# Second mixer: the products between token halves as whole matmuls, those of the two coarsest levels as 64 by 64 tiles

## The chip, the cores and the metric

The kernel runs on one core of one Trainium2 chip. The metric is the device time of one execution in microseconds; the time of the kernel before is 2440.34 us, the median of three runs (2439.63 to 2445.22).

A core has engines that run their own streams of instructions side by side: TensorE (matmuls, PE in the profile; its weight loads stand apart as PEld), VectorE (DVE), ScalarE (ACT), GpSimd (POOL) and SyncE (SP, which here issues most transfers). They meet through semaphores. Matmul results go to PSUM, everything else lies in SBUF, and the weights come from device memory by DMA.

## The reference

The reference is a trunk of two layers over 256 tokens of width 2048, in float32. Each layer adds a token mixer and then a gated MLP with a convolution of width 3; RMS norms stand before each, and one closes the trunk. The first layer's mixer is an mLSTM, the second layer's an HGRN2 recurrence, run forward and backward over the tokens with 16 heads of width 128. The change concerns the second alone:

```python
def _hgrn_chunk(s_st, xs):
    q, k, lf, v = xs
    b = jnp.cumsum(lf, axis=2)
    rel = jnp.where(lower[:, :, None], b[:, :, :, None, :] - b[:, :, None, :, :], -jnp.inf)
    attn = jnp.einsum('bhtsk,bhsk->bhts', jnp.exp(rel) * q[:, :, :, None, :], k)
    o = jnp.einsum('bhts,bhsv->bhtv', attn, v) + jnp.einsum('bhtk,bhkv->bhtv', q * jnp.exp(b), s_st)
    ...
y = hgrn_direction(q, k_f, lf_f, v) + fl(hgrn_direction(fl(q), fl(k_b), fl(lf_b), fl(v)))
```

Every pair of tokens t and s has a weight: the sum over 128 channels of q at t times k at s times the decays of all tokens between them, forward for s before t and backward for s after t. The output of a head is that 256 by 256 matrix times V.

## The kernel before

All large products are streamed. `stream` walks a list of chunks, 1 MB pieces of weights come in through SyncE's queue, ScalarE and VectorE split each piece into a rounded part and a rest (`wh` in L147, `wl` in L148), and TensorE multiplies both with the activations. In chunks of kind "tm" three matmuls of 512 columns follow each other (L192, L193, L194); in chunks of kind "fm" one of 512 and one of 256 (L202, L209). These are the regular matmuls.

Work of the mixer itself is put between them. `side.tick` counts a planned time with every regular matmul and steps generators that have become due (`Side`, L85 to L113). What a generator issues between two regular matmuls is a visit of TensorE here. A scheduler with a simulated clock then makes the final order of each engine's stream: it goes by the program's order, but lets a ready instruction pass one that isn't ready in its simulation. So a transpose of an earlier head (L767) can stand inside a visit.

The second mixer does a head in `head(hd)` (L666 to L751). The decay between two tokens is built by levels of 1, 2, 4, 8, 16, 32 and 64 tokens: at each level VectorE multiplies blocks of the tiles QZ and KZ by a factor from G (L706, L707), GpSimd halves G (L712), and `gather` copies the blocks of a level into a pair of tiles, keys and queries, called kq (L686). After the last level comes the visit. It forms the matrix of weights, keys on partitions and queries on columns:

- between the two halves of 128 tokens, straight from QZ and KZ: four matmuls for each direction, each with 32 keys as the weights and 128 queries as columns, written to 32 partitions of the PSUM tile `pa` (L718 to L723);
- for the two coarsest levels (ms[6] and ms[5]): `product` with 8 matmuls each, 32 keys against 64 queries, to `pa` (L724, L725);
- for the five finer levels and the diagonal (ks and q): `product` with 8 matmuls each, 32 keys against 32 queries, to `pd` (L726 to L728).

Then ScalarE copies `pd` to AD (L729), VectorE puts the levels together under masks (L731), ScalarE copies `pa` to AT (L732) and the diagonal blocks from AD into it (L735). About ten microseconds later four matmuls multiply AT with V (L746), the result is scaled, and `finish` transposes it (L767). The data are float32, which TensorE takes in two passes: one such matmul of the source stands in the profile as two weight loads and two matmuls. The 16 heads follow each other; the visit of a head is one of 16.

Of the kernel before, what the change touches and what calls it, by code (L numbers as in the profile page):

```python
# [15 lines left out]
P = 128  # L16
T = 256
# [31 lines left out]
QUAD = 32  # L49
# [6 lines left out]
def trunk_kernel(ctx, tc, xT, x_d, fg_d, pp_d, cst_d, w_first, w_aq, w_ak, w_av, w_ao, w_aout,  # L56
                 w_bq, w_bv, w_bg, w_bout, w_up, w_down, out, mscr):
    nc = tc.nc
    act, dve, pool, pe = nc.scalar, nc.vector, nc.gpsimd, nc.tensor
# [21 lines left out]
    def aux(name):  # L81
        return psa.tile([P, 512], F32, tag="aux", name=name)
# [283 lines left out]
    def head_scale(ss, width):  # L366
        rs = ev.tile([P, 2], F32, tag="rs", bufs=6, name="rs")
        dve.tensor_scalar(rs, ss, 1.0 / width, EPS, ALU.mult, ALU.add)
        pool.tensor_tensor(rs, rs, hmx, ALU.pow)
        return rs  # L370
# [235 lines left out]
    def hgrn(norm, nxt):  # L606
# [25 lines left out]
        def blocks(z, h, a, b):  # L632
            v = z[:, 0:2 * (T + h)].rearrange("k (p x) -> k p x", p=2)[:, :, a:b]
            return v.rearrange("k p (m j) -> k m p j", j=2 * h)[:, :, :, 0:h]

        def gview(g, n, start, h):
            v = g[:, start:start + 2 * (n - 1)].rearrange("k (p x) -> k p x", p=2)[:, :, 0::2]
            return v.rearrange("k p m -> k m p").unsqueeze(3).broadcast_to([P, n // 2, 2, h])

        def take(hd, what, ps):  # L640
            mp = box["mp"]
            st = heads[hd]
            if what == 0:
                st["q"] = mp.tile([P, T], F32, tag="q", bufs=2, name="q")
                fm_scaled(ps, norm.R, st["q"], box["oml"][:, hd:hd + 1])
                st["QK"] = mp.tile([P, 1152], F32, tag="QK", bufs=2, name="QK")
                st["G"] = mp.tile([P, 768], F32, tag="G0", bufs=2, name="G")
                return
            dr = what - 1
            lb, oml = box["lb"], box["oml"]  # L650
            QZ, KZ, G = st["QK"][:, 0:512], st["QK"][:, 512:1024], st["G"]
            z = mp.tile([P, T], F32, tag="z", bufs=2, name="z")
            fm_scaled(ps, norm.R, z)
            g = G[:, dr * T:(dr + 1) * T]
            kz = KZ[:, dr * T:(dr + 1) * T]
            act.activation(g, z, AF.Sigmoid)
            act.activation(kz, z, AF.Sigmoid, scale=-1.0)
            dve.tensor_scalar(g, g, oml[:, hd:hd + 1], lb[:, hd:hd + 1], ALU.mult, ALU.add)
            pool.tensor_tensor(QZ[:, (1 - dr) * T:(2 - dr) * T], st["q"], g, ALU.mult)
            if dr == 0:  # L660
                pool.tensor_copy(G[:, 512:768], g)
            else:
                st["ks"] = mp.tile([P, T], F32, tag="ks", bufs=2, name="ks")
                pool.tensor_tensor(st["ks"], KZ[:, 0:T], KZ[:, T:2 * T], ALU.add)
                side.push(head(hd))

        def head(hd):
            mp = box["mp"]
            st = heads[hd]
            while hd and "done" not in heads[hd - 1]:  # L670
                yield 0.3
            QZ, KZ = st["QK"][:, 0:640], st["QK"][:, 512:1152]
            q, ks, G = st["q"], st["ks"], st["G"]
            AT = mp.tile([P, 4, P], F32, tag="AT", bufs=2, name="AT")
            AD = mp.tile([P, 2, QUAD], F32, tag="AD", bufs=2, name="AD")

            def gather(h):

                i = box["turn"] % (4 + MIX)
                box["turn"] += 1  # L680
                if i < 4:
                    m = keep.tile([P, 2, T], F32, tag=f"yt{KT - 4 + i}", name=f"kq{i}")
                else:
                    m = mp.tile([P, 2, T], F32, tag="kq", bufs=MIX, name="kq")
                for j, z in enumerate((KZ, QZ)):
                    dve.tensor_copy(m[:, j].rearrange("k (m p j) -> k m p j", p=2, j=h), blocks(z, h, 0, T))  # L686
                return m[:, 0], m[:, 1]

            def product(pd, k, q, n, at):

                for b in range(8):
                    o, c, t = b % 4 * QUAD, b // 4 * pd.shape[1] // 2, at(b)
                    c += t % P if pd.shape[1] == T else 0
                    pe.matmul(pd[o:o + QUAD, c:c + n], k[:, b * QUAD:(b + 1) * QUAD], q[:, t:t + n], start=True, stop=True)  # L694

            def both(ps):
                return ps.rearrange("p (a b) -> p a b", a=2)

            step = SPREAD if hd < BH - 2 else STEP
            mask = [cst[:, C_LV + i * QUAD:C_LV + (i + 1) * QUAD].bitcast(I32).unsqueeze(1).broadcast_to([P, 2, QUAD])  # L700
                    for i in range(FINE)]
            ms, n = [gather(1)], T
            yield step
            for li, h in enumerate(LEVELS):
                qa, ka = blocks(QZ, h, 0, T), blocks(KZ, h, 0, T)
                dve.tensor_tensor(ka, ka, gview(G, n, 1, h), ALU.mult)  # L706
                dve.tensor_tensor(qa, qa, gview(G, n, n + 1, h), ALU.mult)  # L707
                if h < 64:
                    ms.append(gather(2 * h))
                    n //= 2  # L710
                    G2 = mp.tile([P, 3 * n], F32, tag=f"G{h}", bufs=2, name="G2")
                    pool.tensor_tensor(G2, G[:, 0:6 * n:2], G[:, 1:6 * n:2], ALU.mult)  # L712
                    G = G2
                else:
                    st["done"] = True
                yield step
            pa, pd = aux("pa"), aux("pd")
            for b in range(4):  # L718
                o = slice(b * QUAD, (b + 1) * QUAD)
                pe.matmul(pa[o, 2 * P:3 * P], KZ[:, b * QUAD:(b + 1) * QUAD], QZ[:, T + P:2 * T], start=True, stop=True)  # L720
            for b in range(4):
                o, k = slice(b * QUAD, (b + 1) * QUAD), T + P + b * QUAD
                pe.matmul(pa[o, 3 * P:4 * P], KZ[:, k:k + QUAD], QZ[:, 0:P], start=True, stop=True)  # L723
            product(pa[:, 0:T], *ms[6], 64, lambda b: (b // 2 ^ 1) * 64)  # L724
            product(pa[:, 0:T], *ms[5], 64, lambda b: b // 2 * 64)  # L725
            for i in reversed(range(FINE)):  # L726
                product(pd[:, (i + 1) * 64:(i + 2) * 64], *ms[i], QUAD, lambda b: b * QUAD)
            product(pd[:, 0:64], ks, q, QUAD, lambda b: b * QUAD)  # L728
            act.copy(AD, both(pd[:, 0:64]))  # L729
            for i in range(FINE):  # L730
                dve.copy_predicated(AD, mask[i], both(pd[:, (i + 1) * 64:(i + 2) * 64]))  # L731
            act.copy(AT, pa.rearrange("p (a b) -> p a b", a=4))  # L732
            for j in range(4):
                o = slice(j * QUAD, (j + 1) * QUAD)
                act.copy(AT[o, 0:2, o], AD[o])  # L735
            yield
            while "V" not in st["qd"]:
                yield
            V, j = st["qd"]["V"], hd % 4
            py = aux("py")  # L740
            y = mp.tile([P, T], F32, tag="y", bufs=4, name="y")
            ss = mp.tile([P, 2], F32, tag="ss", bufs=2, name="ss")
            for t in range(2):
                c = slice(t * P, (t + 1) * P)
                for s in range(2):
                    pe.matmul(py[:, c], AT[:, s if s == t else 2 + s], V[:, s, j * P:(j + 1) * P], start=(s == 0), stop=(s == 1))  # L746
            act.copy(y, py[:, 0:T])
            for t in range(2):
                jk = ev.tile([P, 512], F32, tag="jk", bufs=1, name="jk")
                act.activation(jk[:, 0:P], y[:, t * P:(t + 1) * P], AF.Square, accum_out=ss[:, t:t + 1])  # L750
            st["y"] = (y, head_scale(ss, 128))  # L751
# [113 lines left out]
    c, close0 = ffn(0, n1, n2)  # L865
    chunks += c
    c = hgrn(n2, n3)
    b = c[0].before
# [6 lines left out]
    c, close1 = ffn(1, n3, nf)  # L875
# [85 lines left out]
```

## Time and profile before

| what | value |
|---|---|
| median of three runs | 2440.34 us (2439.63 to 2445.22) |
| the profiled execution's own time | 2440.68 us |
| its span | 2438.6 us |
| mean granted TensorE clock | 0.998 |
| TensorE busy in the second mixer, 1099 to 1640 us | 537.7 of 541 us |
| VectorE busy there | 456.3 us |
| ScalarE busy there | 283.4 us |
| instruction packets of queue q8 there | 39 of 115 |

The span is the time from the first to the last recorded instruction; the profiled execution's time has 2.1 us around it. The profile names a group of instructions by its line in the kernel, its engine, the tiles it writes and reads, and its shape: `128*32 128x64` is a matmul of 128 rows by 32 columns of weights with 64 columns of data. In a timeline, records of the same kind that follow each other are merged: the row has the first start, the time from it to the last end, and their count. Ends of matmuls are modelled and overlap the next start; starts are measured.

### The profile page before, as it was taken

How to read it: one execution, taken by the hardware profiler on the slowest of the kernel's cores; microseconds unless marked ns; L12 is line 12 of the kernel's file. 1: busy time of each engine (PE TensorE's matmuls, PEld its weight loads, DVE VectorE, ACT ScalarE, POOL GpSimd, SP SyncE). 2: the span in 40 equal slices, each digit the busy share in tenths (PEclk: the TensorE clock that was granted, in tenths of full speed). 3: DMA queues.
4: the chain of work that ended last, by engine and by line, in shares of the span. 5: the costliest groups of instructions: out<-in, count | busy, mean ns of one | idle time of the engine just before them, and what ended most of it. 6: DMA issues, size and time to landing. Idle time of an engine off the chain costs nothing.

```text
span 2438.6 us, 37099 instructions
## 1 busy us (share of the span) xinstructions
PE 2422.2 (99%) x14767; PEld 2068.0 (85%) x14767; DVE 1692.7 (69%) x2768; ACT 1208.0 (50%) x1831; POOL 160.9 (7%) x219
## 2 busy tenths in 40 slices
PE   9999999999999999999999999999999999999998
PEld 7888888888888888888888888888888888888887
DVE  7766556777645777657887988885677754677754
ACT  6655455444434444445554555545544443444443
POOL 0100000000000000001222222220000000000000
PEclk9999999999999999999999999999999999999999
DMA  7654555555555555555544554455555555555554
GB/s 288 199 180 160 186 177 186 190 190 190 191 197 184 188 190 186 183 192 184 173 163 167 173 172 159 172 178 194 183 190 190 190 193 197 185 185 188 190 185 143
DMA packets 66205, 451.90 MB, mean 185 GB/s; under 512 B 7648, under 2 KB 8160, under 8 KB 13424
## 3 DMA queue, kind: packets, MB, share of 16 engines
q1 hardware_dynamic: 63792, 442.91, 53.4%
q0 software_dynamic: 1232, 5.31, 0.9%
q8 instruction: 115, 1.88, 0.3%
q10 hardware_dynamic: 1008, 1.32, 0.2%
q14 instruction: 58, 0.48, 0.1%
HBM read 447.35 MB, written 2.16 MB: 184 GB/s over the span
## 4 chain that ended last, share of the span: by engine, by line
PE 97%; DVE 1%; issue 1%; ACT 0%; DMA 0%; SPq 0%; POOLq 0%; POOL 0%; ACTq 0%
PE mm L202 36%; PE mm L209 18%; PE mm L192 13%; PE mm L194 13%; PE mm L193 13%; PE pn L508 1%; PE pd L694 1%; PE py L746 1%; PE pz L276 0%; DVE wl L148 0%; PE S L494 0%; PE pa L694 0%; DMA raw<-in_w_first 0%; PE pa L720 0%; DVE QK L706 0%
## 5 line engine op out<-in xcount | busy, mean ns | idle before, releaser
L148 DVE TENSOR_TENSOR wl<-raw,wh 128x1024 fp32r<-128x1024 f32 (+1 forms) x848 | 1032.2, 1219 | 594.3 <-ACT wh L147 584.1
L202 PE MATMUL mm<-xt,wh 128*128 128x512 f32 x3776 | 1326.6, 396 | 0.0
L147 ACT CAST wh<-raw 128x1024 fp32r<-128x1024 f32 (+1 forms) x848 | 881.2, 1041 | 879.0 <-PE mm L194 401.6
L209 PE MATMUL mm<-xt,wl 128*128 128x256 f32 x3776 | 1058.1, 280 | 1.8 <-issue 1.8
L202 PEld LDWEIGHTS mm<-xt,wh 128*128 128x128 f32 x3776 | 709.1, 188 | 167.9 <-issue 2.0
L209 PEld LDWEIGHTS mm<-xt,wl 128*128 128x128 f32 x3776 | 712.5, 189 | 2.1
L194 PE MATMUL mm<-wh,g 128*128 128x512 f32 x674 | 262.8, 390 | 0.0
L192 PE MATMUL mm<-wh,g 128*128 128x512 f32 x674 | 262.6, 390 | 0.0
L193 PE MATMUL mm<-wl,g 128*128 128x512 f32 x674 | 262.3, 389 | 0.0
L192 PE MATMUL mm<-wh,xt 128*128 128x512 f32 x512 | 201.2, 396 | 2.7 <-ACT xt L214 2.2
L193 PE MATMUL mm<-wl,xt 128*128 128x512 f32 x512 | 200.9, 392 | 0.4 <-DVE wl L148 0.4
L194 PE MATMUL mm<-wh,xt 128*128 128x512 f32 x512 | 199.9, 392 | 0.0
L219 ACT COPY b<-mm 128x256 f32<-128x256 f32 x237 | 87.8, 370 | 175.4 <-PE mm L209 175.4
L194 PEld LDWEIGHTS mm<-wh,g 128*128 128x128 f32 x674 | 126.5, 188 | 26.6
L193 PEld LDWEIGHTS mm<-wl,g 128*128 128x128 f32 x674 | 126.5, 188 | 26.2
L192 PEld LDWEIGHTS mm<-wh,g 128*128 128x128 f32 x674 | 126.5, 188 | 26.1
L192 PEld LDWEIGHTS mm<-wh,xt 128*128 128x128 f32 x512 | 95.6, 188 | 23.1 <-ACT xt L214 2.9
L193 PEld LDWEIGHTS mm<-wl,xt 128*128 128x128 f32 x512 | 96.5, 188 | 20.0 <-DVE wl L148 0.8
L194 PEld LDWEIGHTS mm<-wh,xt 128*128 128x128 f32 x512 | 96.4, 188 | 19.8
L220 DVE TENSOR_TENSOR a<-mm,b 128x256 f32<-128x256 f32 x86 | 36.5, 425 | 54.3 <-ACT b L219 54.3
L686 DVE COPY kq<-QK 128x256 f32<-128x256 f32 x224 | 70.9, 337 | 0.0
L712 POOL TENSOR_TENSOR G<-G 128x384 f32<-128x384 f32 (+2 forms) x96 | 67.8, 707 | 6.3
(204 smaller groups left out, 1825.4 us busy)
## 6 DMA issues: line engine op xcount, KB each, us to landing
raw<-in_w_up SPq DMA_DIRECT2D x172, 1024.0 KB, 5.0
raw<-in_w_down SPq DMA_DIRECT2D x80, 1024.0 KB, 4.8
raw<-in_w_bq SPq DMA_DIRECT2D x48, 1024.0 KB, 5.0
raw<-in_w_ao SPq DMA_DIRECT2D x16, 1024.0 KB, 4.8
raw<-in_w_aout SPq DMA_DIRECT2D x16, 1024.0 KB, 4.8
raw<-in_w_bv SPq DMA_DIRECT2D x16, 1024.0 KB, 4.8
raw<-in_w_bg SPq DMA_DIRECT2D x16, 1024.0 KB, 4.8
raw<-in_w_bout SPq DMA_DIRECT2D x16, 1024.0 KB, 4.8
```

The lines of the kernel that those rows point to most:

```text
L147: act.copy(wh[:, :m], r)
L148: dve.tensor_tensor(wl[:, :m], r, wh[:, :m].bitcast(F32), ALU.subtract)
L192: pe.matmul(ps[t], xh, wh[:, c], start=st, stop=False)
L193: pe.matmul(ps[t], xh, wl[:, c], start=False, stop=False)
L194: pe.matmul(ps[t], xl, wh[:, c], start=False, stop=sp)
L202: pe.matmul(ps[f], wh[:, c:c + P], x, start=st, stop=False)
L209: pe.matmul(ps[f][:, 0:T], wl[:, c:c + P], x[:, 0:T], start=False, stop=sp)
L219: act.copy(b, ps[:, T:2 * T])
L220: dve.tensor_tensor(dst, ps[:, 0:T], b, ALU.add)
L508: pe.matmul(pn[:, 0:258], w, v, start=(i == 0), stop=(i == len(parts) - 1))
L686: dve.tensor_copy(m[:, j].rearrange("k (m p j) -> k m p j", p=2, j=h), blocks(z, h, 0, T))
L712: pool.tensor_tensor(G2, G[:, 0:6 * n:2], G[:, 1:6 * n:2], ALU.mult)
```

## The change

The four matmuls per direction between token halves become one each, with 128 keys as the weights. `product` gets a width w, 64 for the two coarsest levels and 32 (QUAD) for the others: it walks blocks of w keys, against the w queries of the same block or of its neighbour (`flip`), and writes w partitions. A visit has 2 + 2 x 4 + 6 x 8 = 58 matmuls of the source in place of 4 + 4 + 2 x 8 + 6 x 8 = 72. What is computed for the masked blocks stays the same, and nothing on other engines changes.

```diff
-            def product(pd, k, q, n, at):
-
-                for b in range(8):
-                    o, c, t = b % 4 * QUAD, b // 4 * pd.shape[1] // 2, at(b)
-                    c += t % P if pd.shape[1] == T else 0
-                    pe.matmul(pd[o:o + QUAD, c:c + n], k[:, b * QUAD:(b + 1) * QUAD], q[:, t:t + n], start=True, stop=True)
+            def product(pd, k, q, w, flip=None):
+
+                for b in range(T // w):
+                    o, e = b * w % P, b ^ (flip or 0)
+                    c = b * w // P * pd.shape[1] // 2 + (0 if flip is None else e * w % P)
+                    pe.matmul(pd[o:o + w, c:c + w], k[:, b * w:(b + 1) * w], q[:, e * w:(e + 1) * w], start=True, stop=True)
...
-            for b in range(4):
-                o = slice(b * QUAD, (b + 1) * QUAD)
-                pe.matmul(pa[o, 2 * P:3 * P], KZ[:, b * QUAD:(b + 1) * QUAD], QZ[:, T + P:2 * T], start=True, stop=True)
-            for b in range(4):
-                o, k = slice(b * QUAD, (b + 1) * QUAD), T + P + b * QUAD
-                pe.matmul(pa[o, 3 * P:4 * P], KZ[:, k:k + QUAD], QZ[:, 0:P], start=True, stop=True)
-            product(pa[:, 0:T], *ms[6], 64, lambda b: (b // 2 ^ 1) * 64)
-            product(pa[:, 0:T], *ms[5], 64, lambda b: b // 2 * 64)
+            pe.matmul(pa[:, 2 * P:3 * P], KZ[:, 0:P], QZ[:, T + P:2 * T], start=True, stop=True)
+            pe.matmul(pa[:, 3 * P:4 * P], KZ[:, T + P:2 * T], QZ[:, 0:P], start=True, stop=True)
+            product(pa[:, 0:T], *ms[6], 64, 1)
+            product(pa[:, 0:T], *ms[5], 64, 0)
             for i in reversed(range(FINE)):
-                product(pd[:, (i + 1) * 64:(i + 2) * 64], *ms[i], QUAD, lambda b: b * QUAD)
-            product(pd[:, 0:64], ks, q, QUAD, lambda b: b * QUAD)
+                product(pd[:, (i + 1) * 64:(i + 2) * 64], *ms[i], QUAD)
+            product(pd[:, 0:64], ks, q, QUAD)
```

## The prediction

> **What bounds the kernel now.** I read the page first, then the timeline of one visit on TensorE, then every place where TensorE paused in the second mixer (1099 to 1640 us of the span).
>
> ```profile
> span 2438.6 us, 37099 instructions
> PE 2422.2 (99%) x14767; PEld 2068.0 (85%) x14767; DVE 1692.7 (69%) x2768; ACT 1208.0 (50%) x1831; POOL 160.9 (7%) x219
> ...
> q8 instruction: 115, 1.88, 0.3%
> ...
> PE 97%; DVE 1%; issue 1%; ACT 0%; DMA 0%; SPq 0%; POOLq 0%; POOL 0%; ACTq 0%
> ```
>
> TensorE is the bound: 99% busy, 97% of the chain that ended last. So a nanosecond taken from or added to its stream is a nanosecond of the end, as long as nothing makes it wait. The q8 line comes back below: 115 packets brought instructions. 14767 matmul records and as many weight loads, 29534 together, make 257 to a packet. "Issue", 1% of the chain, is waiting that no operand explains.
>
> A regular visit, from the timeline of TensorE (start us, duration us, line, how many merged):
>
> ```profile
> 1171.03 0.39 PE L193 MATMUL mm<-wl,xt 128*128 128x512 f32 x1
> 1171.26 0.39 PE L194 MATMUL mm<-wh,xt 128*128 128x512 f32 x1
> 1171.58 0.43 PE L720 MATMUL pa<-QK 128*32 128x128 f32 x8
> 1171.82 0.40 PE L723 MATMUL pa<-QK 128*32 128x128 f32 x8
> 1172.04 0.63 PE L694 MATMUL pa<-kq 128*32 128x64 f32 x32
> 1172.48 0.87 PE L694 MATMUL pd<-kq 128*32 128x32 f32 x78
> ...
> 1173.20 0.32 PE L694 MATMUL pd<-q,ks 128*32 128x32 f32 x14
> 1173.45 0.50 PE L192 MATMUL mm<-wh,xt 128*128 128x512 f32 x1
> 1173.79 0.40 PE L193 MATMUL mm<-wl,xt 128*128 128x512 f32 x1
> ```
>
> Starts are what count here, since the ends overlap. Each 32-wide matmul of the source stands there as two passes (four in L720 give x8). From the last regular matmul (1171.26) to the second regular one after the visit (1173.79) pass 2.53 us: 0.32 to the first product, 0.24 + 0.22 for the token halves, 0.44 for the two coarsest levels, 0.97 for the finer ones and the way back, 0.34 until the second regular one. Regular matmuls start 0.23 apart, so going from 128-wide to 32-wide tiles costs 0.32 - 0.23 = 0.09, and the first load afterwards is exposed too (0.24 against 0.22: 0.02). The way back exposes a 128-wide load: 0.34 against 0.23, that is 0.11.
>
> **What the edits cost.** No transfer is moved, and no instruction of another engine is added or taken. Work on ScalarE that reads the two PSUM tiles starts up to 0.15 us later; ScalarE is 50% busy, and without that cover each visit would pay the 0.15 once more.
>
> Token halves: eight 32-wide matmuls (16 passes) become two whole ones (4 passes). Four narrow tiles evidently work at once, so 16 passes took 0.46. The price of whole f32 passes of 128 columns is in the later products with V, and the switch from one to 32-wide tiles is at another visit, which a transpose (L767) cuts in two:
>
> ```profile
> L746 PE MATMUL py<-V,AT 128*128 128x128 f32 x128 | 17.5, 275 | 0.0
> ...
> 1198.85 1.05 PE L746 MATMUL py<-V,AT 128*128 128x128 f32 x8
> ...
> 1251.50 0.27 PE L767 MATMUL pz<-cst,y 128*128 128x128 f32 x1
> 1251.70 0.41 PE L720 MATMUL pa<-QK 128*32 128x128 f32 x2
> 1252.03 0.33 PE L767 MATMUL pz<-cst,y 128*128 128x128 f32 x1
> ...
> 1254.15 0.39 PE L209 MATMUL mm<-xt,wl 128*128 128x256 f32 x1
> ```
>
> Eight passes in 1.05, the last one 0.275 long (the mean in the first row, from the groups by line): (1.05 - 0.275) / 7 = 0.111 apart. Four of them are 0.44, the narrow ones 0.46: no gain in throughput, whatever the count says. What goes is the switch on entering (0.09). It comes back at once at the next edge: from a whole pass to narrow tiles takes 0.20 (1251.50 to 1251.70). So to the first 64-wide pass it is 0.23 + 3 x 0.111 + 0.20 = 0.76, where it was 0.32 + 0.46 = 0.78.
>
> Two coarsest levels: 16 matmuls (32 passes, four at a time, 0.44) become 8 of twice the width (16 passes). The trace shows no 64-wide tile. If two halves work side by side, as the four quarters do, each pair of passes lasts what four quarters last (0.44 / 8 = 0.055): again 0.44. If they take turns it is 16 x 0.055 = 0.88. I take 0.44, since quarters and whole tiles both deliver full width. The first load behind the switch is exposed, between 0.02 (32 wide) and 0.11 (128 wide); I take 0.05.
>
> A new edge, from 64-wide to 32-wide tiles: below, nothing; above, the switch of 0.09 and the 0.02 of the load. I take the upper, 0.11, because the only change of width that the trace shows costs that.
>
> A visit then has 0.76 + 0.49 + 0.11 + 0.97 + 0.34 = 2.67 against 2.53: +0.15 us unrounded, x16 visits = **+2.4 us**. Bounds: -0.3 (no second switch, loads hidden) and +9.4 (halves in turn).
>
> The transposes: at 1251.70 a whole-width transpose between narrow products made the visit 2.45 long (to 1254.15) instead of 1.87 (1171.58 to 1173.45); less its own 0.11 that is 0.47. One more visit has the same cut. Between whole products it would switch nothing: -0.9 if both still fall there, 0 if the scheduler puts them among narrower ones. I take **-0.5**.
>
> **The pauses.** TensorE stood still three times for nothing that it computes with:
>
> ```profile
> 1316.39 0.40 PE L202 MATMUL mm<-xt,wh 128*128 128x512 f32 x1
> 1318.58 0.28 PE L209 MATMUL mm<-xt,wl 128*128 128x256 f32 x1 [1.79 <-issue]
> ...
> 1322.22 0.28 PE L209 MATMUL mm<-xt,wl 128*128 128x256 f32 x1
> 1322.34 0.40 PE L202 MATMUL mm<-xt,wh 128*128 128x512 f32 x1
> 1322.58 0.28 PE L209 MATMUL mm<-xt,wl 128*128 128x256 f32 x1
> ```
> ```profile
> 1485.34 0.89 PE L694 MATMUL pd<-kq 128*32 128x32 f32 x78
> 1487.57 0.22 PE L694 MATMUL pd<-kq 128*32 128x32 f32 x1 [1.34 <-issue]
> ...
> 1625.76 0.57 PE L694 MATMUL pd<-q,ks 128*32 128x32 f32 x14
> ```
> ```profile
> 1318.60:1322.20 3.60, 3.60 (x12) 3.06 (x12) 2.12 (x4) 2.55 (x7) 0.00 (x0) 0.53 0.02 5
> 1445.00:1470.00 25.00, 25.00 (x146) 22.02 (x145) 19.74 (x36) 14.02 (x28) 7.38 (x11) 1.00 0.46 157
> 0.00:1317.50 1317.50, 1312.60 (x7629) 1119.68 (x7630) 904.56 (x1470) 667.43 (x1009) 70.31 (x104) 1.00 0.56 189
> 0.00:1487.00 1487.00, 1480.24 (x9160) 1263.57 (x9160) 1049.61 (x1759) 755.33 (x1168) 122.07 (x169) 1.00 0.55 186
> 0.00:1625.90 1625.90, 1618.50 (x10563) 1382.07 (x10563) 1171.78 (x2017) 828.95 (x1306) 157.17 (x214) 1.00 0.55 185
> ```
>
> The window rows give TensorE's busy time with its count, then that of the loads, of the other engines, the granted clock and the DMA load. The first pause is 2.19 - 0.23 = 1.96; behind it the granted clock is 0.53, and six pairs take 3.64 (1318.58 to 1322.22) where a pair takes 0.36: 1.5 more. The second: the last of the 78 began at about 1486.0 (their end less one pass of 0.2), the next at 1487.57: 1.5. The third: the closing 14 passes take 0.57 instead of 0.32, 0.25. Together 5.2.
>
> Their places are the evidence. Matmuls plus loads before them: 15259, 18320, 21126. The steps are 3061 and 2806, which is 12 x 256 and 11 x 256 less 11 and 10 semaphore instructions that these rows don't count. TensorE paused each time at the end of a 256-instruction block, and q8 brings about 257 to a packet. The cause I read: a visit has 8 + 8 + 32 + 96 = 144 passes, with their loads 288 instructions, in 1.9 us: more than a block, where ordinary work uses 291 in 25 us. When a block begins just as a visit does, the visit eats it before the next arrives. From the visit ahead of the first pause (1313.9) to the release (1318.6) are 4.7 us: the most that a refill needs. In 4.7 us the old stream wants 288 + 2.8 x 11.6 = 320 instructions, 64 more than there are. The new visit has 2 x (4 + 16 + 96) = 232, and the stream wants 232 + 2.7 x 11.6 = 263: seven too many at the worst alignment, some 0.6 us, seldom. So the change takes away **-5.2 us**, though nothing in its arithmetic is quicker.
>
> [...]
>
> **Sum.** Profiled execution 2440.7 + 2.4 - 0.5 - 5.2 = **2437.4 us**. It lies 0.3 above the median 2440.34, so against that median it is 0.1% down. 0.3% (7.3 us) is about what a measurement of this kernel can tell from no change: below 2433.0 is faster, above 2447.7 slower.
>
> **Rivals.**
> 1. The pauses stay, or come at other block ends. For it: all alignments shift, and only three were seen. Against it: the instruction count above. 2440.7 + 2.4 - 0.5 = 2442.6. [...]
> 2. 64-wide halves take turns: 16 x 0.44 = 7.0 more, 2444.4; with rival 1 as well, 2449.6.
> 3. Slower than before through the order: the scheduler lets transposes pass into visits, and each that lands between narrow tiles costs 0.47. L767 transposes twice for each of 16 heads, 32 in all. With both present cuts kept, the sum is 2437.9, and six more make it slower than before; one more in every visit gives 2445.4, and 0.3% needs 21 more. For it: it happened at 1252.03. Against it: nearly all visits are whole today.
> 4. Quicker than I sum: no second switch (-0.3 in place of +2.4), both transposes free (-0.9): 2434.3. And the finer products run at (0.87 - 0.2) / 77 = 8.7 ns a pass, where half of a 64-column pass (0.44 / 32 = 13.8 ns) would be 6.9; if a shorter run of instructions ahead lets them go at that pace, 96 x 1.8 ns x 16 = 2.8 more, 2431.5. Against it: the one switch that is seen. [...]
>
> **Chances.** Forecast 0.50, rival 1 0.12, rival 2 0.12, rival 3 0.08, rival 4 0.18. Faster by over 0.3%: two thirds of rival 4 (towards its lower sum) and 0.05 of the forecast's own spread, together 0.17. Slower: the half of rival 2 that comes with rival 1 (0.06), half of rival 3 (0.04) and 0.02 for waits that a new order could bring, 0.12. Same: 0.71. The range reaches from between rival 4's two sums to rival 2's: 2432.5 to 2444.5.
>
> **What would show it.** Right: first whole pass 0.23 behind the last regular matmul and four whole passes 0.11 apart; 0.20 to the first 64-wide; 16 passes of those in 0.44 to 0.5; about 0.1 lost before the 32-wide; visits 1.9 to 2.1 long; no "issue" pause in the mixer; three or four q8 packets fewer (16 x 56 / 256 = 3.5). Wrong: a pause of over 1 us at a multiple of 256 instructions, 64-wide passes starting singly 0.055 apart, or a transpose among narrow tiles in many visits.

## The result, and the profile after

The changed kernel takes 2436.59 us (median; 2436.1 to 2438.23) against 2440.53 us for the kernel before, run beside it. The ratio is 0.9983, with a 95% interval from 0.9976 to 0.9991: 0.17% down, 3.9 us. That is within the 0.3% that the prediction called no change, inside its range, and 0.8 us under its 2437.4 us. The profiled execution took 2436.56 us, that of before 2440.68.

From the page of the changed kernel:

```profile
span 2434.7 us, 36201 instructions
PE 2421.4 (99%) x14319; PEld 2069.5 (85%) x14319; DVE 1691.8 (69%) x2768; ACT 1207.5 (50%) x1831; POOL 160.7 (7%) x219
...
q8 instruction: 112, 1.84, 0.3%
...
PE 99%; ACT 0%; DMA 0%; issue 0%; DVE 0%; SPq 0%; POOLq 0%; POOL 0%
```

TensorE has 448 passes fewer (14319 in place of 14767, 28 for each of 16 visits) and three instruction packets of q8 fewer (112 in place of 115), but its busy time is nearly the same: 2421.4 us in place of 2422.2. "Issue" has gone from 1% to 0% of the chain. So the time was not gained by multiplying less.

The visit that answers to the one at 1171.58 before, on the timeline of TensorE:

```profile
1171.39 0.40 PE L194 MATMUL mm<-wh,xt 128*128 128x512 f32 x1
1171.63 0.39 PE L718 MATMUL pa<-QK 128*128 128x128 f32 x2
1171.85 0.39 PE L719 MATMUL pa<-QK 128*128 128x128 f32 x2
1172.16 0.69 PE L694 MATMUL pa<-kq 128*64 128x64 f32 x16
1172.78 0.86 PE L694 MATMUL pd<-kq 128*32 128x32 f32 x78
...
1173.74 0.50 PE L192 MATMUL mm<-wh,xt 128*128 128x512 f32 x1
1174.08 0.40 PE L193 MATMUL mm<-wl,xt 128*128 128x512 f32 x1
```

From the last regular matmul (1171.39) to the second one after the visit (1174.08) pass 2.69 us; before it was 2.53. A visit has become 0.15 to 0.16 longer. 0.24 pass to the first whole product, 0.53 to the 64-wide ones (1172.16), 0.62 to the 32-wide ones, 0.96 until the way back, 0.34 to the second regular matmul.

What was gained lies between the instructions. The busy time of each engine in the mixer, first before and then after (TensorE is the first number behind the length):

```profile
1099.00:1640.00 541.00, 537.72 (x4952) 460.50 (x4951) 456.29 (x929) 283.39 (x508) 139.35 (x177) 1.00 0.50 171
```
```profile
1099.00:1640.00 541.00, 541.00 (x4522) 465.34 (x4521) 458.44 (x931) 284.53 (x510) 139.88 (x178) 1.00 0.50 172
1295.00:1320.00 25.00, 25.00 (x345) 21.64 (x344) 20.14 (x48) 13.31 (x27) 0.70 (x1) 1.00 0.50 169
1470.00:1495.00 25.00, 25.00 (x228) 21.19 (x227) 24.96 (x58) 12.76 (x22) 9.37 (x10) 1.00 0.50 169
```

Before, TensorE stood idle for 3.3 us of this stretch; after, for nothing. The stretches that held the two long pauses (1316 and 1486 us) are full and at full clock.

### The profile page after: what moved, and what is told of

It is laid out like the page before. It is cut to its first block, busy times and chain, and to the rows that moved or that the text cites. A ratio compares the mean times of both kernels' runs of the same rounds, so it can differ in the third digit from the quotient of the medians.

```text
span 2434.7 us, 36201 instructions
## 1 busy us (share of the span) xinstructions
PE 2421.4 (99%) x14319; PEld 2069.5 (85%) x14319; DVE 1691.8 (69%) x2768; ACT 1207.5 (50%) x1831; POOL 160.7 (7%) x219
## 4 chain that ended last, share of the span: by engine, by line
PE 99%; ACT 0%; DMA 0%; issue 0%; DVE 0%; SPq 0%; POOLq 0%; POOL 0%
PE mm L202 36%; PE mm L209 18%; PE mm L192 13%; PE mm L194 13%; PE mm L193 13%; PE pn L508 1%; PE pd L694 1%; PE py L742 1%; PE pz L276 0%; PE pa L694 0%; PE S L494 0%; DMA raw<-in_w_first 0%; PE pz L763 0%; ACT xt L214 0%; PE pa L719 0%
```

## The experiments

All ratios are against the kernel before on the same chip. TensorE's idle time is taken from the busy time in the same stretch, 1099 to 1640 us of each profile.

| kernel | instructions in a visit | time, us | ratio (95%) | TensorE idle in the mixer, us |
|---|---|---|---|---|
| before | 288 | 2440.5 to 2441.4 | 1 | 3.3 |
| after | 232 | 2436.59 | 0.9983 (0.9976 to 0.9991) | 0 |
| e1: before, half a block on | 288 | 2439.48 | 0.9991 (0.9982 to 1.0) | 2.5 |
| e2: after, padded | 288 | 2445.76 | 1.0016 (1.0006 to 1.0025) | 2.4 |
| e3: whole halves alone | 264 | 2434.12 | 0.9971 (0.9959 to 0.9982) | 0 |
| e4: 64-wide levels alone | 256 | 2440.02 | 0.9994 (0.9985 to 1.0003) | 0 |
| e6: after, at the worst block ends | 232 | 2436.74 | 0.9984 (0.9974 to 0.9993) | 0 |
| e7: e3, at the worst block ends | 264 | 2437.25 | 0.9986 (0.9977 to 0.9995) | 1.9 |
| e8: e3 again | 264 | 2433.87 | 0.9970 (0.9959 to 0.998) | 0 |
| e9: after again | 232 | 2436.74 | 0.998 (0.9971 to 0.9989) | 0 |

The theory, inferred from the 0.09 us that one edge of width took, from pauses at steps of 256 instructions and from about 257 to a q8 packet: a visit is lengthened a little by its switches of tile width, and the pauses are TensorE waiting for the next block of its own instructions, so that they depend on how many instructions a visit has and where block ends fall in it. The rival for the pauses: these visits wait for their data. The rival for the visit: width costs by itself.

### e1: the same kernel, half a block further on

The kernel before, with tiny matmuls added ahead of the first regular one, where TensorE is idle for 1.74 us before the change:

```diff
     for _ in range(8):
         pe.matmul(idle[:, 0:P], ones[:, 0:P], ones[:, 0:P], start=True, stop=True)
+    for _ in range(32):
+        pe.matmul(idle[0:QUAD, P:P + 8], ones[:, 0:QUAD], ones[:, 0:8], start=True, stop=True)
```

> The kernel before with 32 tiny matmuls more (64 passes, 128 instructions) while TensorE is idle in the first microseconds, so that every later instruction lies half a block of 256 further on. Theory (the pauses are instruction refills): the pauses leave visits 6, 11 and 16 and come at others. Counted from the block ends that the three pauses mark, the sixteen visits of before begin 177, 127, 83, 46, 13, 215, 171, 134, 105, 48, 4, 225, 194, 137, 93 and 240 instructions into a block, and it paused at 215, 4 and 240. Half a block on, visits 2 (255), 3 (211), 8 (6), 9 (233), 14 (9) and 15 (221) stand in that danger zone: two to five of them pause by 0.2 to 2.0 us, visits 6, 11 and 16 don't; time 2437 to 2443 us. Rival (the pauses belong to what these visits wait for): visits 6, 11 and 16 pause as before, 2440.5 us.

The pauses moved. Visits 6, 11 and 16 no longer pause; visits 8, 9 and 15 do, by 0.4, 1.3 and 1.3 us. The two longer ones on the timeline, and the counts before each of them (TensorE, then its loads):

```profile
1423.19 0.26 PE L694 MATMUL pd<-q,ks 128*32 128x32 f32 x9
1424.60 0.26 PE L694 MATMUL pd<-q,ks 128*32 128x32 f32 x5 [1.14 <-issue]
...
1608.61 0.50 PE L192 MATMUL mm<-wh,xt 128*128 128x512 f32 x1
1610.23 0.39 PE L193 MATMUL mm<-wl,xt 128*128 128x512 f32 x1 [1.12 <-issue]
```
```profile
0.00:1424.20 1424.20, 1422.15 (x8649) 1214.74 (x8650) 998.62 (x1656) 723.51 (x1110) 104.48 (x147) 1.00 0.54 187
0.00:1609.50 1609.50, 1606.66 (x10435) 1373.49 (x10436) 1158.08 (x1981) 821.08 (x1289) 156.86 (x213) 1.00 0.54 185
```

The counts are 17299 and 20871, their distance 3572: 14 blocks of 256 less 12. From the first pause before the change (15259) to 17299 it is 8 blocks less 8. The rows leave out semaphore instructions; the traces record 12 more of TensorE's at the second of these counts than at the first, and 8 more at 17299 than at 15259, so that the distances are whole blocks. So the grid of block ends stays where it was in the stream, and other visits have moved onto it; the rival, that visits 6, 11 and 16 wait for their data, falls. Of the six visits named, three paused; visits 2, 3 and 14 (255, 211 and 9 instructions into a block) did not.

### e2: the changed kernel with the old number of instructions

```diff
             product(pd[:, 0:64], ks, q, QUAD)
+            for b in range(14):
+                o = b % 4 * QUAD
+                pe.matmul(pd[o:o + QUAD, 448:456], ks[:, 0:QUAD], q[:, 0:8], start=True, stop=True)
```

> The changed kernel with 14 tiny 32-wide matmuls more in each visit (28 passes, 56 instructions), whose result nothing reads: a visit has 288 instructions again, as before the change. The passes themselves cost 28 x 8.5 ns x 16 = 3.8 us: 2440.4 us. Theory (refills): with the old count the block ends fall where they fell before the change, and visits 6, 11 and 16, or two of them, pause again by 0.2 to 2 us; with the slow clock behind a pause 3 to 5 us more, 2443.5 to 2445.5 us. Rival (the pauses went because of the wider tiles or another order): no pause, 2440.4 us.

2445.76 us, 9 us above the changed kernel and 0.3 above the range expected. The profiled execution, the fastest of ten, took 2443.16, 6.6 above the changed kernel's: the added passes make some 3.7 of it (an ordinary visit is 0.22 to 0.24 us longer) and the two pauses below 2.7. Behind the first of them the pairs of regular matmuls start 0.35 apart, as at full clock, and the other 2.6 us of the median are not explained. The pauses are back behind visit 6 and in visit 11; visit 16 has none:

```profile
1318.24 0.40 PE L202 MATMUL mm<-xt,wh 128*128 128x512 f32 x1
1320.25 0.28 PE L209 MATMUL mm<-xt,wl 128*128 128x256 f32 x1 [1.61 <-issue]
```
```profile
1487.69 0.28 PE L727 MATMUL pd<-q,ks 128*32 128x8 f32 x9
1488.73 0.33 PE L727 MATMUL pd<-q,ks 128*32 128x8 f32 x18 [0.77 <-issue]
```
```profile
0.00:1319.50 1319.50, 1314.28 (x7629) 1121.96 (x7630) 904.69 (x1470) 667.27 (x1009) 70.21 (x104) 1.00 0.55 189
0.00:1488.40 1488.40, 1481.99 (x9160) 1266.76 (x9161) 1049.88 (x1759) 755.05 (x1168) 121.92 (x169) 1.00 0.54 186
```

The counts are the striking part: 7629 and 7630 at the first pause, 9160 and 9161 at the second. Before the change the rows had 7629 and 7630, 9160 and 9160. The tile widths are others, and in visit 11 another matmul was under way when it happened, and yet TensorE stops behind the same instruction number (within one). The wider tiles didn't prevent the pauses with 288 instructions a visit; with the same tiles and 232 there was none.

### e3: whole token halves alone

The kernel before, of which only the first part of the diff is taken:

```diff
-            for b in range(4):
-                o = slice(b * QUAD, (b + 1) * QUAD)
-                pe.matmul(pa[o, 2 * P:3 * P], KZ[:, b * QUAD:(b + 1) * QUAD], QZ[:, T + P:2 * T], start=True, stop=True)
-            for b in range(4):
-                o, k = slice(b * QUAD, (b + 1) * QUAD), T + P + b * QUAD
-                pe.matmul(pa[o, 3 * P:4 * P], KZ[:, k:k + QUAD], QZ[:, 0:P], start=True, stop=True)
+            pe.matmul(pa[:, 2 * P:3 * P], KZ[:, 0:P], QZ[:, T + P:2 * T], start=True, stop=True)
+            pe.matmul(pa[:, 3 * P:4 * P], KZ[:, T + P:2 * T], QZ[:, 0:P], start=True, stop=True)
```

> Only the token halves are sent whole, the two coarsest levels stay 32 wide: no 64-wide tiles, so one switch fewer than the changed kernel. A visit: 0.23 + 0.53 + 0.02 + 0.44 + 0.97 + 0.34 = 2.53 us from the last regular matmul to the second after it, as before the change (2.53), and 0.15 less than in the changed kernel. It has 2 x (4 + 32 + 96) = 264 instructions, so a pause is still possible where a block ends just at a visit's start; by the count that is visits 4, 8 and 12 (230, 222 and 217 into a block), 0 to 1.5 us each. Theory: 2440.5 - 5.2 (old pauses) - 0.9 (transposes between whole products) = 2434.4 without pauses, up to 2437 with them. Rival (the width of the tiles costs or gains by itself, not through switches): whole halves bring nothing or lose, 2440 to 2442 us.

2434.12 us: faster than both kernels. There is no pause, not in visits 4, 8 and 12 either, and the visit is 2.55 us long (1171.27 to 1173.82):

```profile
1171.27 0.40 PE L194 MATMUL mm<-wh,xt 128*128 128x512 f32 x1
1171.50 0.39 PE L718 MATMUL pa<-QK 128*128 128x128 f32 x2
1171.72 0.39 PE L719 MATMUL pa<-QK 128*128 128x128 f32 x2
1172.04 0.65 PE L694 MATMUL pa<-kq 128*32 128x64 f32 x32
1172.51 0.87 PE L694 MATMUL pd<-kq 128*32 128x32 f32 x78
...
1173.48 0.50 PE L192 MATMUL mm<-wh,xt 128*128 128x512 f32 x1
1173.82 0.39 PE L193 MATMUL mm<-wl,xt 128*128 128x512 f32 x1
```

The 32 narrow passes of the two coarsest levels, now the first behind an edge of width, take 0.47 (1172.04 to 1172.51) where they took 0.44. In the changed kernel the 16 passes of twice the width take 0.62: the first pair leads the second by 0.106 where the others are 0.058 apart, and another switch follows, 0.09. That is the whole difference between the two visits.

### e4: 64-wide levels alone

The changed kernel with the token halves put back to eight 32-wide matmuls, that is, the diff of e3 the other way round.

> Only the two coarsest levels become 64 wide, the token halves stay 32 wide. Two switches more than before the change (32 to 64 and back to 32), each 0.09 and an exposed load of 0.05 and 0.02: a visit of 2.53 + 0.25 = 2.78 us, 4.0 us over the 16. 256 instructions a visit: pauses become rare and short (0 to 2 us in all). Theory: 2440.5 + 4.0 - 5.2 = 2439.3, up to 2441.5 with a pause. Rival (no cost for a switch between narrow widths): a visit of 2.55, 2435.5 us.

2440.02 us, 0.7 above the 2439.3 expected without a pause; why is not shown. The visit is 2.80 us, with a switch between 32 and 64 on each side of the 64-wide products:

```profile
1171.29 0.39 PE L194 MATMUL mm<-wh,xt 128*128 128x512 f32 x1
1171.61 0.43 PE L720 MATMUL pa<-QK 128*32 128x128 f32 x8
1171.85 0.40 PE L723 MATMUL pa<-QK 128*32 128x128 f32 x8
1172.18 0.69 PE L694 MATMUL pa<-kq 128*64 128x64 f32 x16
1172.80 0.86 PE L694 MATMUL pd<-kq 128*32 128x32 f32 x78
...
1174.09 0.39 PE L193 MATMUL mm<-wl,xt 128*128 128x512 f32 x1
```

Behind L723 come 0.33 us where before the change there were 0.22: 0.11 for a switch between two narrow widths, where the one from the full width took 0.09. So 64-wide tiles cost 0.27 us a visit by the edges that they bring, and their only gain here is 32 instructions fewer. That was enough to end the pauses where its block ends fell; no run moved them.

### e6 and e7: luck or margin

If fewer instructions only moved the block ends to kinder places, the changed kernel would be no better than e1. So the changed kernel (e6) and e3 (e7) were each put where the most visits meet a block end, with tiny matmuls at the start as in e1, here over four tiles in turn (the 64 passes of e1, all on one, took 3.58 us):

```diff
+    for i in range(47):   # e7: 60
+        o = i % 4 * QUAD
+        pe.matmul(idle[o:o + QUAD, P:P + 8], ones[:, 0:QUAD], ones[:, 0:8], start=True, stop=True)
```

> The changed kernel with 47 tiny matmuls (188 instructions) in the idle first microseconds, so that five of its sixteen visits begin where the kernel before paused: visits 2, 5, 10, 13 and 15 at 3, 233, 244, 222 and 9 instructions into a block. Theory (a visit of 232 instructions is shorter than a block of 256, and the refill comes back in time): no pause above 0.6 us anywhere, 2436.6 us plus 0 to 1 us for the later start. Rival (the changed kernel was only lucky in where its block ends fell): two or more of these visits pause by 0.5 to 2 us, 2438.5 to 2443 us.

> The kernel with whole token halves alone (264 instructions a visit) with 60 tiny matmuls (240 instructions) in the idle first microseconds: visits 3, 4, 8, 11, 12 and 15 then begin 19, 218, 210, 4, 201 and 253 instructions into a block. Theory: 264 is more than a block, so visits that begin within a few instructions of a block's start can still pause: visit 11 or 15, or both, by 0.4 to 2 us, the others not; 2434.5 to 2438 us. Rival (it is safe like the changed kernel, whatever the block ends): no pause, 2434.1 us plus 0 to 1 us for the later start.

The changed kernel has a margin: five visits begin at a block end, TensorE is busy for all 541 us of the stretch, and the time is 2436.74. e3 has none, as expected of 264 instructions: visit 15 (253 instructions into a block) pauses for 1.4 us, and against the expectation there is one of 0.8 behind visit 12 (201), none at visit 11 (4). In e7:

```profile
1504.88 0.28 PE L209 MATMUL mm<-xt,wl 128*128 128x256 f32 x1
1505.81 0.39 PE L202 MATMUL mm<-xt,wh 128*128 128x512 f32 x1 [0.65 <-issue]
...
1606.14 0.28 PE L694 MATMUL pd<-q,ks 128*32 128x32 f32 x11
1607.65 0.25 PE L694 MATMUL pd<-q,ks 128*32 128x32 f32 x3 [1.23 <-issue]
```
```profile
0.00:1505.60 1505.60, 1502.53 (x9414) 1285.74 (x9415) 1071.19 (x1812) 768.54 (x1197) 122.72 (x170) 1.00 0.56 187
0.00:1607.20 1607.20, 1603.14 (x10307) 1372.49 (x10308) 1158.01 (x1981) 820.78 (x1288) 157.00 (x213) 1.00 0.55 186
```

18829 and 20615 instructions, 1786 apart, 7 blocks less 6, and 6 semaphore instructions lie between. It takes 2437.25 us, so e3's lead over the changed kernel is gone once its block ends fall badly.

### e8 and e9: the two side by side

e3 and the changed kernel unaltered, on one chip.

> The kernel with whole token halves alone once more, beside the changed kernel on one chip. Theory: two switches of tile width in a visit instead of three, 0.15 us less in each visit: 2434.1 us, 2.4 us under the changed kernel. Rival (the gap seen so far belongs to the chip): no more than 1 us under it.

> The changed kernel itself, beside the kernel with whole token halves alone on one chip: 2436.6 us, no pause.

2433.87 against 2436.74 us: 2.9 us, where the edges of a visit say 16 x 0.14 = 2.2 and 2.4 was expected; the rest is not explained. The version with whole token halves and nothing else is the best found, as long as the stream ahead of it stays as it is.

## Why the prediction was right

*What bounds.* TensorE's stream set the time before (97% of the chain) and after (99%); every term below is time in that stream.

*Token halves: no gain in throughput.* Right. The whole passes are 0.11 apart, 0.22 from L718 to L719, and it takes 0.77 us to the first 64-wide pass where 0.76 was worked out.

*Two coarsest levels.* Right: 16 passes in two halves side by side. In the trace they start two by two, 0.01 apart, and the pairs 0.058 apart (0.055 was taken), the second pair 0.05 later than that. 0.62 from the first to the first 32-wide pass was summed as 0.49 + 0.11 = 0.60. Rival 2, halves that take turns, would have shown 1.0 (16 x 0.055 and the same edges).

*The new edge.* The upper bound was taken, and it was nearly that: the step from the last pair to the first 32-wide pass is 0.15 us, 0.09 more than from pair to pair. e4 shows the same a second time. With it the lower sum of rival 4 falls. Its other part falls too: the finer products and the way back take 0.96 us where they took 0.97, although fewer instructions stand ahead of them.

*+2.4 us for the visits.* 2.69 against 2.53 in the visit shown, with +0.15 in unrounded starts: 2.4.

*Transposes, -0.5.* This term was too small: it was set half way between 0 and -0.9. Both cut visits became whole, because the scheduler now lets the two transposes of a head stand side by side ahead of the products. The timeline of the changed kernel at the visit that was cut at 1252.03:

```profile
1252.14 0.40 PE L202 MATMUL mm<-xt,wh 128*128 128x512 f32 x1
1252.38 0.38 PE L763 MATMUL pz<-cst,y 128*128 128x128 f32 x2
1252.60 0.39 PE L718 MATMUL pa<-QK 128*128 128x128 f32 x2
...
1254.71 0.39 PE L209 MATMUL mm<-xt,wl 128*128 128x256 f32 x1
```

From the first transpose to the regular matmul it is 2.33 us (1252.38 to 1254.71), where it was 2.65 (1251.50 to 1254.15): 0.32 less although a visit is 0.15 longer, so 0.47 for each of two, -0.9 beside the +2.4 already counted. They stand so in e3 too, but not in e4, so it is the whole token halves that bring this order. The mechanism named was another (a transpose between whole products, at no switch); what happened was a new order. The prediction overlooked a third cut visit: in visit 16 a transpose stands among the products of the coarse levels (at 1624.30 before); it still does, at 0.1 us less. So rival 3 had its ground, but the cut visits became fewer, not more.

*The pauses, -5.2 us.* Right in size and, as far as the runs show it, in cause. The regular matmuls follow each other in the same order in both profiles, so their starts tell where time was gained: 3.5 us between visits 6 and 7, where the first pause and the slow clock stood, and, apart from the +0.15, 1.55 in visit 11 and 0.25 in visit 16 (without the 0.1 by which its transpose became cheaper), together 5.3. e1, e2 and e7 tie the pauses to the count of instructions. Rival 1 falls by e6, and the seven instructions too many that the prediction worked out for the worst alignment didn't show there.

Each pause left TensorE idle for 0.2 to 2.0 us (before, e1, e2 and e7). Blocks of 256 fit every pause seen: from one pause of before to the next TensorE's records, its semaphore instructions among them, number 3072 and 2816, exactly 12 and 11 x 256. That TensorE waits there for the block's arrival is inferred from this and from the packets below; no run delayed a packet alone.

With -1.0 for the three cut visits in place of -0.5, and -5.3 for the pauses, the sum is 2436.8 for the profiled execution, which took 2436.6. What is left, 0.2 us, is not explained.

Which of the visits at a block end pauses can be read from the instruction packets of q8, if they are paired with the blocks in order. In each of the ten pauses TensorE went on 2.3 to 2.7 us after the packet of the new block had begun (2.46, 2.37 and 2.28 in before), and in all ten profiles no block of the second mixer began sooner than 2.27 us after its packet. Visits 2 and 14 of e1 and 11 of e7 didn't pause: their packets had begun 2.7, 3.2 and 4.7 us ahead of the block. In visit 3 of e1 it was 2.3 us, just in time; the block behind visit 12 of e7 had a packet that began only 2.4 us before TensorE went on. The shortest of these times is 4.1 us in the changed kernel and 5.0 in e6, which is its margin; e3 has 3.0 and, run again in e8, 2.6, and e4, with 2.4, only just got by. What stays open is what makes a packet begin early or late: no run here separates that.

## What to carry to other kernels

Where one engine is full, look for its pauses marked "issue" and count its instructions up to each: a common step, 256 here, pointed to its running out of instructions. Here visits of 264 and more instructions in about 2 us paused in some places, and visits of 232 in none (after, e6). Narrow tiles side by side gave the throughput of a whole tile (0.46 against 0.44 us for the token halves), so what counts here in choosing a width is the number of switches (0.09 to 0.11 us each, and 0.02 to 0.11 more by the first step behind them) and of instructions; take the widest where it saves both, and leave two neighbours at the same width where only a switch would be added. And price a change in pieces: the two parts of this one were worth -6.4 to -7.3 and -0.5 to -1.4 us against the kernel before (the second not clear of noise), and together, at -3.9, less than the first alone. Each part alone already ended the pauses where its block ends fell, so that gain can't be counted twice.

## What the runs showed that was not expected

The slow clock doesn't follow every pause. Behind the 1.96 us pause before the change the granted clock was 0.53 for 3.6 us; behind the 1.8 us pause of e2 (1318.24 to 1320.25) the next pairs of regular matmuls take 0.35, as at full speed. The time of two kernels that pause is less steady, too: the runs of the kernel before lie between 2438.7 and 2446.3 us, e2's between 2443.2 and 2447.3, those of the changed kernel between 2436.1 and 2438.2. But e1's, with three pauses, lie between 2438.7 and 2440.1, so a pause alone doesn't explain it.
